# Where the first norm of a transformer trunk is applied: before three projections, or at their read-out

## The chip, the cores and the metric

The kernel runs on one core of a Trainium2 chip. Its time is device microseconds (us) of one execution; the median of three runs of the kernel before is 1945.42 us (1943.68 to 1946.59). The engines are named as the profile names them: PE multiplies matrices (PEld is its weight load, which overlaps), DVE does elementwise arithmetic, ACT does scaled copies and activations, POOL is a slower elementwise engine, and SP issues most DMA transfers from one queue, in order. Each engine works through its own instructions in the order in which the program holds them, and waits on semaphores for the others.

## The reference, cut to what matters

Two layers of a transformer with 512 latent and 256 context tokens of width 1024. Each layer starts like this (float32):

```python
def rms_norm(x, g):
    y = x * lax.rsqrt(jnp.mean(x * x, axis=-1, keepdims=True) + EPS)
    return y * g
def modulate(h, shift, scale):
    return h * (1 + scale) + shift

mod = silu(c) @ w_mod[l] + b_mod[l]          # one vector for latents, one for context
h   = modulate(rms_norm(x, norm1[l]), shift, scale)
z   = h @ w_in[l]                            # keys, values, queries of two kinds of attention, two gates
```

So for a token t and a channel c, `h = x[t,c] * r[t] * A[c] + m[c]`, where `r[t]` is the norm's factor of the token, `A[c] = norm1[c] * (1 + scale[c])`, and `m[c]` is the shift. `A` and `m` come in two sets, one for latents and one for context. A projection is `h @ W = r[t] * ((x*A) @ W) + m @ W`: the factor of a token can be taken out of the sum over channels, and the shift adds one number per output channel.

## The kernel before, in words

All tensors lie with the channels on 128 partitions and the tokens along the free axis: 8 tiles `x[k]` of 128 channels by 768 tokens (512 latents, then 256 context; spans s=0 and s=1). A float32 product is made of three matmuls: an operand is split into a high part rounded to `fp32r` and the low part that is left, and the terms high*high, low*high and high*low are added in PSUM. So a projection of 128 output channels takes 8 k by 3 matmuls over 512 columns and 8 by 3 over 256. The weights are split in the same way: `wh` by ACT (L640 for the stream of later weights, `wr` being the raw ones) and `wl` by POOL (L642).

The front of layer 0 is written in `Trunk.start`. It loads `x` (L840), squares each tile (`square`, ACT L844), adds the squares (`total`, DVE L847), sums them over the partitions by a matmul with ones (`means`, PE L853), adds eps, raises to the power -1/2 on POOL, and spreads the factor over all partitions with a matmul (`widen`, PE L870), so that it lies in PSUM as `rb`. Meanwhile the 8 column blocks of `w_mod` come in, two transfers of 512 KB each (`fetch`, L631, sixteen in all); for each k `sums` (PE L891), `parts` (ACT L897), `choose` (PE L901) and `settle` (DVE L906 and L909) make `A[:, :, k]` and `mod[:, :, k]`. Until there is something to multiply, PE runs matmuls that nothing uses (`warm`, L836). Then `scaled` (DVE L915) turns `x[k]` into x*A*r in place, `high` (ACT L920) writes `h` and `low` (DVE L924) writes `hl`. `multiply` (PE L950) runs the three projections whose weights are loaded first: gk (the keys), gv (the values) and gq0 (the first two query heads) of the grouped-query attention.

Behind the front come generators that read the projections out: `evac` of gk takes squares and a copy with the gain (ACT L1073, L1074) and sums the squares per head on PE (`st`, L1062); gv's is turned (`tv`, PE L1149). After them PE runs "fillers", projections that wait for nothing but weights and `h` (L655): nk0 (the keys of the first neighbourhood heads), nv0 (values), nq0 and so on; ACT L1200 and DVE L1201 read nk0's out. Between the fillers come the scores of the grouped-query attention, `sc` (L1305).

What sets the order: in the front, `Ops.run` plans a list of operations with costs in us, engine and priority (lower goes first), and sorts every engine's instructions by the planned starts. `FIRST` gives the order of the loads (x = a token tile, w = weights of a projection, b = small tables, a digit = the two halves of `w_mod` for that k). The fillers' instructions and loads are put in between and behind by a planner that reads the numbers in `PLAN[0]`. In PSUM, there are 8 banks; names `pj` are banks of projections. When the front is over, the mixing stage's pools g, t, s are laid over the same banks, in the order that `banks` gives, and a bank's new user waits until the old one has been read.

Of the kernel before, what the change touches and what calls it, by code (L numbers as in the profile page):

```python
# [12 lines left out]
F32 = mybir.dt.float32  # L13
# [7 lines left out]
P = 128  # L21
D = 1024
KB = D // P
# [21 lines left out]
for _n in ORDER:  # L45
    for _j in range(COLS[_n][1]):
# [32 lines left out]
         busy=12, ctx=0.0, vat=(1, 1), load=2, qt=2, rx=2, slow=(1.1, 1.2, 1), banks="gst", lead=(2, 1, 2), quiet=0.0, spared=0, all=False),  # L79
# [7 lines left out]
FIRST = "x x x x x x x x b 0 w 1 2 w 3 w 4 5 6 7"  # L87
AHEAD = 9

HOWW = "vvv"  # L90
START, HOP, LAND = 4.06, 0.15, 0.25
# [512 lines left out]
class Trunk:  # L604
# [207 lines left out]
    def start(self, h, pool, others):  # L812
# [8 lines left out]
        pick = pool.tile([P, 2], F32, tag="pick", name=self.name("pick"))  # L821
        nc.gpsimd.memset(cols, 0.0)
# [4 lines left out]
        tiles, x, sqs, rb, raws = {}, [], [], {}, {}  # L827
# [4 lines left out]
        add = todo.add  # L832
        chosen = self.ps("n", "ch")

# [11 lines left out]
        def total(k):  # L846
            nc.vector.tensor_tensor(sqs[0], sqs[0], sqs[k], op=ALU.add)  # L847

        def means(k):
            if k == 0:  # L850
                tiles["st"] = self.ps("n", "st")
            for t in range(nt):
                nc.tensor.matmul(  # L853
                    tiles["st"][:, t : t + 1], sqs[k][:, t * P : (t + 1) * P], self.ones, start=(k == 0 and t == 0),
                    stop=(k > 0), skip_group_check=True)

        def eps():
            r = tiles["r"] = pool.tile([P, nt], F32, tag="rs", name=self.name("rs"))
            nc.vector.tensor_scalar(r, tiles["st"][:, :nt], EPS, None, op0=ALU.add)
# [6 lines left out]
        def widen(s):  # L866
            a, b = spans[s]
            rb[s] = self.ps("n", "rb")
            for t in range(a // P, b // P):
                nc.tensor.matmul(  # L870
                    rb[s][:, t * P - a : t * P - a + P], tiles["r"][:, t : t + 1].to_broadcast([P, P]), self.ident,
                    start=True, stop=True)
# [38 lines left out]

        def scaled(k, s):
# [25 lines left out]
        def wlow(i, eng):  # L938
            weights[i].append(self.wpool.tile([P, D], F32R, tag="wl", name=self.name("wl")))
            (nc.gpsimd if eng == "g" else nc.vector).tensor_tensor(  # L940
                weights[i][2], weights[i][0], weights[i][1][:].bitcast(F32), op=ALU.subtract)

        def multiply(i, s, k):
            if k == 0:
                self.ahead[i, s] = self.ps("a", "pj")
            a, b = spans[s]
            ps, (raw, whi, wlo) = self.ahead[i, s][:, : b - a], weights[i]
            c = slice(k * P, (k + 1) * P)
            for n, (u, v) in enumerate(((whi, h[0]), (whi, h[1]), (wlo, h[0]))):
                nc.tensor.matmul(ps, u[:, c], v[k][:, a:b], start=(k == 0 and n == 0), stop=(k == KB - 1 and n == 2))  # L950
# [5 lines left out]
        last = None  # L956
        for what in FIRST.split():
            if what == "x":
                k = len(loaded)
                loaded.append(add("d", 0.92, token, (k,), [], 1))  # L960
                sq = add("a", 0.77, square, (k,), [loaded[k]], 1)
                if k < KB - 1:
                    last = add("v", 0.87, total, (k,), [last, sq], 1) if k else sq
                    continue
                last = add("p", 1.34, means, (0,), [last], 0)
                last = add("v", 0.08, eps, (), [add("p", 1.34, means, (KB - 1,), [last, sq], 0)], 0)
                wide = [
                    add("p", c, widen, (s,), [add("g", g, power, (s,), [last], 0)], 0)
                    for s, c, g in ((0, 0.86, 0.96), (1, 0.43, 0.63))]
# [1675 lines left out]
```

## Time and profile before

| what | value |
|---|---|
| median of three runs | 1945.42 us (1943.68 to 1946.59) |
| the profiled execution | 1943.38 us |
| its span in the trace | 1940.7 us |
| PE busy | 1909.2 us, 98% of the span |
| DVE busy | 1471.7 us, 76% |
| ACT busy | 937.8 us, 48% |
| POOL busy | 227.5 us, 12% |
| granted PE clock | 0.998 of full speed |

The times in the trace count from the start of the span. In a row of the timeline stand the start in us, the busy time in us, the engine, the line, the operation, out<-in, shapes, and the number of instructions that were put together; in brackets how long the engine was idle before it and what ended that. In a row of the windows stand the stretch, and for each engine its busy us and the number of its instructions, then the granted clock, the share of the DMA engines that was busy, and GB/s.

### The profile page before, as it was taken

The page shows a single profiled execution, that of the slowest core. Times are in us where ns is not written, and L with a number is a line of the kernel's source. Part 1 is how long each engine was busy: PE and PEld are TensorE (multiplying, and loading weights), DVE is VectorE, ACT ScalarE, POOL GpSimd, SP SyncE. Part 2 cuts the span into 40 slices and gives each one's busy share as a digit, 9 for nine tenths or more (in the row PEclk, how much of TensorE's full clock was granted, in tenths as well). Part 3 has the DMA queues.
Part 4 walks back from the last instruction along what each step waited for, and adds up shares of the span by engine and source line. Part 5 has one row for each costly group of instructions (what it writes and reads, how often), then busy time and mean ns, then how long its engine had stood idle before and what let it go on. Part 6 is the DMA issues. An engine that isn't in the chain of part 4 may idle for free.

```text
span 1940.7 us, 31522 instructions
## 1 busy us (share of the span) xinstructions
PE 1909.2 (98%) x12300; PEld 1764.5 (91%) x12300; DVE 1471.7 (76%) x2797; ACT 937.8 (48%) x1820; POOL 227.5 (12%) x132
## 2 busy tenths in 40 slices
PE   8999999999999999999999999999999999999998
PEld 6989999898889999999999888889988999999998
DVE  6468887769777888787868578898557587877785
ACT  4456666642226533343424345666553355544553
POOL 0432212214300000000000012132210000000000
PEclk9999999999999999999999999999999999999999
DMA  8121112235462134334443411022145532332332
GB/s 328 46 69 42 53 58 63 77 120 179 158 217 87 66 109 130 109 120 131 139 144 131 152 55 33 34 79 82 55 128 175 199 109 77 98 120 90 104 96 83
DMA packets 71670, 210.85 MB, mean 109 GB/s; under 512 B 8545, under 2 KB 10721, under 8 KB 71521
## 3 DMA queue, kind: packets, MB, share of 16 engines
q1 hardware_dynamic: 71520, 208.84, 32.9%
q8 instruction: 96, 1.57, 0.3%
q14 instruction: 54, 0.43, 0.1%
HBM read 196.75 MB, written 6.82 MB: 105 GB/s over the span
## 4 chain that ended last, share of the span: by engine, by line
PE 64%; DVE 5%; issue 1%; ACT 1%; DMA 1%; POOL 0%; SPq 0%; DVEq 0%; POOLq 0%; ACTq 0%
PE po L655 21%; PE qu L2021 14%; PE qv L2021 7%; PE pj L540 4%; PE qc L2021 3%; PE pj L655 3%; PE pf L655 3%; PE pp L655 2%; PE sc L540 2%; PE y L540 2%; PE tp L540 1%; PE pv L540 1%; ACT p L540 1%; DVE m L540 1%; DVE ptl L540 0%
## 5 line engine op out<-in xcount | busy, mean ns | idle before, releaser
L2021 PE MATMUL qu<-r,w 128*128 128x384 f32 (+1 forms) x1872 | 295.9, 310 | 0.3
L2021 PEld LDWEIGHTS qu<-r,w 128*128 128x128 f32 x1872 | 281.0, 189 | 5.0 <-DVE tt L2501 3.8
L1884 ACT ACTIVATE w<-wr 128x512 fp32r<-128x512 f32 x234 | 145.5, 625 | 107.6 <-DVE wr L2465 36.2
L655 PE MATMUL po<-ph,wh 128*128 128x512 f32 (+1 forms) x576 | 197.4, 343 | 0.0
L655 PE MATMUL po<-ph,wl 128*128 128x512 f32 (+1 forms) x576 | 196.8, 342 | 0.0
L655 PE MATMUL po<-pl,wh 128*128 128x512 f32 (+1 forms) x576 | 196.2, 341 | 0.0
L655 PE MATMUL pj<-h,wh 128*128 128x512 f32 (+1 forms) x512 | 182.1, 356 | 1.4 <-DVE ql L1256 1.1
L655 PE MATMUL pj<-h,wl 128*128 128x512 f32 (+1 forms) x512 | 176.8, 345 | 0.9 <-POOL wl L642 0.9
L655 PE MATMUL pj<-hl,wh 128*128 128x512 f32 (+1 forms) x512 | 176.6, 345 | 0.0
L1876 DVE SCALAR_TENSOR_TENSOR x<-po,G,x 128x256 f32<-128x256 f32 (+3 forms) x168 | 99.2, 596 | 100.7 <-PE po L655 99.7
L1888 DVE TENSOR_TENSOR w<-wr,w 128x512 fp32r<-128x512 f32 x234 | 159.3, 685 | 11.3 <-ACT w L1884 10.3
L640 ACT ACTIVATE wh<-wr 128x1024 fp32r<-128x1024 f32 (+1 forms) x109 | 101.3, 933 | 137.2 <-PE po L655 30.4
L2021 PE MATMUL qv<-r,w 128*128 128x384 f32 (+1 forms) x936 | 150.6, 309 | 0.3 <-ACT tt L2027 0.3
L2021 PEld LDWEIGHTS qv<-r,w 128*128 128x128 f32 x936 | 141.2, 190 | 0.5 <-ACT tt L2027 0.5
L782 POOL TENSOR_TENSOR rs<-rs,expo 128x2 f32<-128x2 f32 (+2 forms) x7 | 5.5, 784 | 1099.8 <-DVE rs L781 1099.8
L642 POOL TENSOR_TENSOR wl<-wr,wh 128x1024 fp32r<-128x1024 f32 (+1 forms) x47 | 103.5, 2205 | 229.2 <-ACT wh L640 228.9
L655 PEld LDWEIGHTS po<-ph,wl 128*128 128x128 f32 x576 | 108.2, 188 | 14.4 <-DVE wl L2192 0.4
L655 PEld LDWEIGHTS po<-pl,wh 128*128 128x128 f32 x576 | 108.5, 188 | 12.8
L655 PEld LDWEIGHTS po<-ph,wh 128*128 128x128 f32 x576 | 108.5, 188 | 12.8
L722 DVE CUSTOM_DVE_ANT_0 wr<-wr,crow 128x1024 f32<-128x1024 f32 x80 | 100.2, 1252 | 14.3 <-DMA wr<-wmodT 14.0
L655 PEld LDWEIGHTS pj<-h,wl 128*128 128x128 f32 x512 | 96.8, 189 | 13.4 <-POOL wl L642 1.3
L655 PEld LDWEIGHTS pj<-h,wh 128*128 128x128 f32 x512 | 97.0, 189 | 11.9 <-PE tp L1331 1.1
(341 smaller groups left out, 4705.7 us busy)
## 6 DMA issues: line engine op xcount, KB each, us to landing
wr<-wfi SPq DMA_DIRECT2D x88, 512.0 KB, 3.2
wr<-wmodT SPq DMA_DIRECT2D x80, 512.0 KB, 3.4
wr<-win SPq DMA_DIRECT2D x68, 512.0 KB, 3.7
wr<-wfo SPq DMA_DIRECT2D x64, 256.0 KB, 2.7
wr<-wo SPq DMA_DIRECT2D x26, 512.0 KB, 4.1
wr<-wmod SPq DMA_DIRECT2D x16, 512.0 KB, 9.9
wr<-wp SPq DMA_DIRECT2D x32, 256.0 KB, 2.9
x<-x SPq DMA_DIRECT2D x16, 384.0 KB, 7.1
```

The source lines that it names most:

```text
L540: ops[i]["run"](*ops[i]["args"], **ops[i]["kw"])
L640: nc.scalar.activation(hi, raw, AF.Copy)
L642: (eng or nc.gpsimd).tensor_tensor(lo, raw, hi[:].bitcast(F32), op=ALU.subtract)
L655: nc.tensor.matmul(ps[:, : b - a], u[:, c], v[k][:, a:b], start=(k == 0 and i == 0), stop=(k == nk - 1 and i == 2),)
L722: self.nc.vector.tensor_tensor_reduce(junk if s else w, w, crow[:, s], 1.0, 0.0, ALU.mult, ALU.add, self.mod[l][:, s, n : n + 1])
L782: nc.gpsimd.tensor_tensor(r[:, :nb], r[:, :nb], self.expo[:, :nb], op=ALU.pow)
L1876: self.nc.vector.scalar_tensor_tensor(x[j][:, f:u], ps[:, f - a : u - a], self.G[l][i][:, s, j : j + 1], x[j][:, f:u], op0=ALU.mult, op1=A ...
L1884: self.nc.scalar.activation(t[:, :n], src, AF.Copy)
L1888: self.nc.vector.tensor_tensor(t[:, n : 2 * n], src, t[:, :n].bitcast(F32), op=ALU.subtract)
L2021: nc.tensor.matmul(banks[bank], u[:, c], v, start=(first and k == 0 and i == 0), stop=(k == kn - 1 and i == 2), skip_group_check=True)
```

## The change

`FIRST` now interleaves loads of tokens with those of `w_mod` and weights. `multiply` (now L975) no longer takes `h`, but tiles made by two new functions: `upper` (ACT L923) and `lower` (DVE L930) split x*A, without `r`, into high and low parts. The context's high part lies in a tile `side` of 260 columns: 256 tokens, and four columns for the shift `m` of latents and context, high and low. So the shift's product with the weights comes out as columns 256 to 259 of the context's bank. All six banks (three projections, two spans) are open at once and are filled k by k. The factor is spread three times over two tiles of tokens and copied into SBUF (`settled`, ACT L878); it is then in the tile `rb`.

At the read-out, `shifts` (DVE L980, L981) adds the two columns of each shift, `normed` (DVE L987) multiplies a bank by the factor into a tile `up`, and `shifted` (ACT L992) adds the shift; the old read-outs take `up` in place of the bank. `h` is still needed by all fillers: `scaled` (DVE L940), `high` (ACT L945) and `low` (DVE L949) make it in the places where x*A stood, each piece when the three projections have used it. All `wl` of the first three projections are made on DVE, as before.

```diff
-         busy=12, ctx=0.0, vat=(1, 1), load=2, qt=2, rx=2, slow=(1.1, 1.2, 1), banks="gst", lead=(2, 1, 2), quiet=0.0, spared=0, all=False),
+         busy=14, ctx=8.0, vat=(1, 1), load=2, qt=2, rx=2, slow=(1.1, 1.2, 1), banks="gts", lead=(2, 1, 2), quiet=0.0, spared=0, all=False),
-FIRST = "x x x x x x x x b 0 w 1 2 w 3 w 4 5 6 7"
-AHEAD = 9
-START, HOP, LAND = 4.06, 0.15, 0.25
+FIRST = "b 0 x w w w 1 x 2 x x 3 x x x x 4 5 6 7"
+SIDE, SIDES = 260, 5
+AHEAD = 8
+START, HOP, LAND = 3.9, 0.15, 0.25
...
+        banks = {(i, s): self.ps("a", "pj") for i in range(3) for s in range(2)}
...
+        def settled(n):
+            if n == 0:
+                tiles["rb"] = pool.tile([P, T], F32, tag="qt", name=self.name("rb"))
+                for s, (a, b) in enumerate(spans):
+                    rb[s] = tiles["rb"][:, a:b]
+            nc.scalar.activation(tiles["rb"][:, n * 256 : n * 256 + 256], chosen[:, 256:512], AF.Copy)
...
+        def upper(k, s):
+            a, b = spans[s]
+            if s:
+                side[k] = pool.tile([P, SIDE], F32R, tag="side", name=self.name("side"))
+            to = side[k][:, 0:CTX] if s else h[0][k][:, a:b]
+            nc.scalar.activation(to, x[k][:, a:b], AF.Copy, scale=self.A[0][0][:, s, k : k + 1])
+            if s:
+                nc.scalar.activation(side[k][:, CTX : CTX + 2], mod[:, :, k], AF.Copy)
+
+        def lower(k, s):
+            a, b = spans[s]
+            hi = side[k][:, 0:CTX] if s else h[0][k][:, a:b]
+            nc.vector.scalar_tensor_tensor(
+                h[1][k][:, a:b], x[k][:, a:b], self.A[0][0][:, s, k : k + 1], hi.bitcast(F32),
+                op0=ALU.mult, op1=ALU.subtract)
+            if s:
+                nc.vector.tensor_tensor(
+                    side[k][:, CTX + 2 : CTX + 4], mod[:, :, k], side[k][:, CTX : CTX + 2].bitcast(F32), op=ALU.subtract)
...
         def multiply(i, s, k):
+            ps, (raw, whi, wlo) = banks[i, s], weights[i]
+            c = slice(k * P, (k + 1) * P)
+            if s:
+                pairs = (whi, side[k][:]), (whi, h[1][k][:, S:T]), (wlo, side[k][:])
+            else:
+                pairs = (whi, h[0][k][:, 0:S]), (whi, h[1][k][:, 0:S]), (wlo, h[0][k][:, 0:S])
+            for n, (u, v) in enumerate(pairs):
+                nc.tensor.matmul(
+                    ps[:, : v.shape[1]], u[:, c], v, start=(k == 0 and n == 0), stop=(k == KB - 1 and n == 2),
+                    skip_group_check=True)
+
+        def shifts(i):
+            nc.vector.tensor_copy(plus[:, i], banks[i, 1][:, CTX : CTX + 2])
+            nc.vector.tensor_tensor(plus[:, i], plus[:, i], banks[i, 1][:, CTX + 2 : CTX + 4], op=ALU.add)
+
+        def normed(i, s):
+            a, b = spans[s]
+            if not s:
+                scaled_up[i] = pool.tile([P, T], F32, tag="qt", name=self.name("up"))
+            nc.vector.tensor_tensor(scaled_up[i][:, a:b], banks[i, s][:, : b - a], rb[s][:, : b - a], op=ALU.mult)
+
+        def shifted(i, s):
+            a, b = spans[s]
+            u = scaled_up[i][:, a:b]
+            nc.scalar.activation(u, u, AF.Identity, bias=plus[:, i, s : s + 1])
+            self.ahead[i, s] = u
...
-            self.pbufs = dict(a=3, n=3, m=2)
+            self.pbufs = dict(a=6, n=1, m=1)
```

How the change moves instructions on three engines. **SP's queue**: `wr...<-wmod0` is half of a block of `w_mod`, `wr...<-win` is a raw weight of a projection (the fillers' in these rows), `x` a token tile. Before, all eight token tiles stand ahead of the first `w_mod`, and then:

```order
L631 DMA wr68_374<-wmod0 128x1024
L631 DMA wr93_668<-win 128x1024
L631 DMA wr102_702<-win 128x1024
L631 DMA wr70_387<-wmod0 128x1024
L631 DMA wr73_400<-wmod0 128x1024
L631 DMA wr76_418<-wmod0 128x1024
L631 DMA wr78_428<-wmod0 128x1024
L631 DMA wr80_446<-wmod0 128x1024
```

Now (the weight of the first filler, wr103, stands a few rows ahead of this piece):

```order
L631 DMA wr51_261<-wmod0 128x1024
L631 DMA wr106_737<-win 128x1024
L631 DMA wr109_743<-win 128x1024
L631 DMA wr116_809<-win 128x1024
L843 DMA x52_272<-x 128x768
L843 DMA x54_287<-x 128x768
L631 DMA wr57_297<-wmod0 128x1024
L631 DMA wr60_311<-wmod0 128x1024
L843 DMA x61_325<-x 128x768
L843 DMA x64_344<-x 128x768
L843 DMA x66_353<-x 128x768
L843 DMA x69_365<-x 128x768
```

Three weights of fillers that stood among or behind the last `w_mod` transfers stand ahead of six token tiles; the last token tile has 8 halves of `w_mod` and 7 weights ahead of it.

**DVE, at the end of the front**, between the last settle and the first read-out of nk0 (`pj112` is nk0's bank of latents, `pj23` to `pj26` are gv's and gq0's banks). Before, the last rows ahead of the read-outs are:

```order
L906 TENSOR_SCALAR A0_0_103<-ch20_137,more1_111,norms_sb_87 128x2
L909 TENSOR_SCALAR mod0_101<-ch20_137,more1_111 128x2
L924 SCALAR_TENSOR_TENSOR hl17_134<-x32_194,mod0_101,h16_133 128x256
L915 SCALAR_TENSOR_TENSOR x34_203<-x34_203,A0_0_103,rb48_265 128x512
L915 SCALAR_TENSOR_TENSOR x34_203<-x34_203,A0_0_103,rb50_272 128x256
L924 SCALAR_TENSOR_TENSOR hl19_136<-x34_203,mod0_101,h18_135 128x512
L924 SCALAR_TENSOR_TENSOR hl19_136<-x34_203,mod0_101,h18_135 128x256
L1048 STREAM_SHUFFLE sh118_792<-qg89_558 128x512
```

Now, where gq0's context bank `pj26` is read last:

```order
L981 TENSOR_TENSOR plus4_114<-plus4_114,pj24_141 128x2
L949 SCALAR_TENSOR_TENSOR hl20_137<-x69_365,mod0_101,h19_136 128x512
L949 SCALAR_TENSOR_TENSOR hl18_135<-x66_353,mod0_101,h17_134 128x256
L949 SCALAR_TENSOR_TENSOR hl20_137<-x69_365,mod0_101,h19_136 128x256
L987 TENSOR_TENSOR up98_680<-pj23_140,rb81_444 128x512
L987 TENSOR_TENSOR up98_680<-pj24_141,rb81_444 128x256
L980 COPY plus4_114<-pj26_143 128x2
L981 TENSOR_TENSOR plus4_114<-plus4_114,pj26_143 128x2
L987 TENSOR_TENSOR up99_686<-pj25_142,rb81_444 128x512
L987 TENSOR_TENSOR up99_686<-pj26_143,rb81_444 128x256
L1260 TENSOR_TENSOR k113_774<-pj112_749,k113_774 64x512
```

Between the last settle and nk0's read-out (now L1260) there were five elementwise passes over tiles; now there are the whole second half of the making of `h` and six read-outs.

**ACT, ahead of the fillers' weights** (L640 makes `wh104`, nk0's high weight). Before, it stands behind the first read-outs:

```order
L1074 ACTIVATE qg89_558<-pj84_515,qgain_99 128x512
L640 ACTIVATE wh94_670<-wr93_668 128x1024
L1073 ACTIVATE sq86_531<-pj88_554 128x256
L1074 ACTIVATE kg85_530<-pj88_554,gain_sb_88 128x256
L640 ACTIVATE wh103_704<-wr102_702 128x1024
```

Now:

```order
L945 ACTIVATE h13_130<-x61_325,mod0_101 128x512
L945 ACTIVATE h5_122<-x30_169,mod0_101 128x256
L945 ACTIVATE h7_124<-x45_236,mod0_101 128x256
L945 ACTIVATE h15_132<-x64_344,mod0_101 128x512
L945 ACTIVATE h9_126<-x52_272,mod0_101 128x256
L945 ACTIVATE h11_128<-x54_287,mod0_101 128x256
L945 ACTIVATE h17_134<-x66_353,mod0_101 128x512
L640 ACTIVATE wh104_733<-wr103_731 128x1024
L640 ACTIVATE wh107_739<-wr106_737 128x1024
L992 ACTIVATE up95_636<-up95_636,plus4_114 128x512
```

nk0's weight was split behind read-outs of the finished banks; it now stands behind `h17`, the high part of `h` for k = 6, which waits for DVE's `scaled` of that tile.

On PE the order within the front is now k by k over all six banks. Behind the front nk0 stood after the sums `st` and the turning `tv`; it now stands directly behind the last `multiply`, ahead of both. nk0's bank of latents takes the place of gk's bank of latents, and nk0's bank of context (`pj115`) takes the place of gq0's bank of context, `pj26`; the bank of nv0's first read-out takes the place of nk0's bank of latents.

123 lines of the change are left out of this document (65 added, 58 removed).

## The prediction

> **What bounds the kernel now.** I read the page's totals first, then the windows of the front, then the timeline of the rows that the change touches.
>
> ```profile
> span 1940.7 us, 31522 instructions
> PE 1909.2 (98%) x12300; PEld 1764.5 (91%) x12300; DVE 1471.7 (76%) x2797; ACT 937.8 (48%) x1820; POOL 227.5 (12%) x132
> ```
>
> PE is busy 98% of the span, so the time can only move by what PE waits: 31.5 us in all, and in the front what it does for nothing. The program behind the first 330 us is the same in both kernels' orders, so whatever the front gains or loses arrives at the end as it is.
>
> ```profile
> core 0: us, PE busy (x) PEld busy (x) DVE busy (x) ACT busy (x) POOL busy (x), PEclk, DMA share, GB/s
> 0.00:5.00 5.00, 1.34 (x6) 1.35 (x7) 1.44 (x13) 1.64 (x3) 0.52 (x5) 1.00 0.49 142
> 5.00:10.00 5.00, 5.00 (x27) 5.00 (x27) 1.92 (x2) 3.23 (x4) 0.00 (x0) 1.00 0.97 347
> 10.00:15.00 5.00, 5.00 (x47) 5.00 (x47) 4.16 (x7) 3.38 (x4) 0.00 (x0) 1.00 1.05 396
> 15.00:20.00 5.00, 5.00 (x52) 4.28 (x51) 1.40 (x2) 1.44 (x2) 1.83 (x2) 1.00 1.02 415
> 20.00:25.00 5.00, 4.07 (x49) 2.53 (x48) 2.59 (x8) 2.47 (x5) 0.00 (x0) 1.00 1.03 420
> 25.00:30.00 5.00, 4.83 (x40) 3.84 (x41) 4.63 (x12) 3.35 (x6) 0.00 (x0) 1.00 1.02 419
> 30.00:35.00 5.00, 4.10 (x37) 2.12 (x35) 5.00 (x12) 2.02 (x4) 0.00 (x0) 1.00 1.03 415
> 40.00:45.00 5.00, 5.00 (x38) 3.82 (x38) 4.96 (x13) 1.79 (x4) 0.00 (x0) 1.00 0.52 213
> 45.00:60.00 15.00, 15.00 (x95) 13.58 (x95) 3.67 (x7) 6.82 (x12) 4.58 (x2) 1.00 0.00 1
> 90.00:112.00 22.00, 20.75 (x134) 18.49 (x133) 17.07 (x40) 15.84 (x34) 7.20 (x3) 1.00 0.31 96
> 160.00:180.00 20.00, 19.42 (x140) 17.97 (x140) 16.52 (x41) 14.68 (x32) 4.65 (x2) 1.00 0.08 28
> 180.00:300.00 120.00, 119.94 (x824) 110.09 (x823) 101.20 (x205) 76.83 (x162) 32.47 (x19) 1.00 0.17 53
> ```
>
> The reader is to see three regimes. Up to 40 us the DMA engines are full (share about 1.0, some 415 GB/s), and PE waits on them. From 45 to 60 us PE has no gap at all and DVE is nearly idle: 3.67 us of 15. Later PE waits little: 1.25 us in 90 to 112, 0.58 in 160 to 180, 0.06 in 180 to 300, which is 1.89 together.
>
> ```profile
> 3.65 11.58 PE L836 MATMUL ch<-ident_sb 128*128 128x128 f32 x76 [3.65 <-DMA ident_sb<-ident]
> 9.14 4.74 ACT L844 ACTIVATE sq<-x 128x768 f32<-128x768 f32 x5 [0.29 <-DMA x<-x]
> 13.70 0.96 DVE L847 TENSOR_TENSOR sq<-sq,sq 128x768 f32<-128x768 f32 x1
> 15.07 2.74 PE L853 MATMUL st<-ones,sq 128*128 128x1 f32 x24
> 19.16 1.60 PE L870 MATMUL rb<-ident_sb,rs 128*128 128x128 f32 x12
> ```
>
> Before, the norm is done early: means at 15.07, the factor spread by 20.8. The 11.58 us of L836 ahead of it are dummies. That idle head is what the change could use; the price is that the factor comes later.
>
> **The change part by part. (A) The projections' end.** The last token tile now follows 8 halves of `w_mod` (4.19 MB) and 7 weights (3.67), itself and its seven fellows being 3.15 MB; with the identity (128x128 f32, 0.07 MB) that is 11.0 MB. The windows' rates, times 5 us each, give 0.71 + 1.74 + 1.98 + 2.08 + 2.10 + 2.10 = 10.7 MB by 30 us, so the last tile is there at about 31, plus 1.1: before, 3.22 MB had passed by 12.0 at these rates and the last square ran from 13.04 (9.14 + 4.74 less a fifth of it). With a square of 0.84 and a total of 0.96 behind it in DVE's queue, and some queueing of 1, the means start near 35 and, half as many as before (1.4 us), end near 36.5.
>
> What PE has left in its order then comes from these rows:
>
> ```profile
> 39.13 0.40 PE L950 MATMUL pj<-h,wl 128*128 128x512 f32 x1
> 39.36 0.40 PE L950 MATMUL pj<-h,wh 128*128 128x512 f32 x1
> 40.49 1.07 PE L891 MATMUL mp<-wr,cols 128*32 128x256 f32 x16
> 42.99 0.50 PE L901 MATMUL ch<-pick,part 128*128 128x2 f32 x4
> 53.00 0.28 PE L950 MATMUL pj<-h,wh 128*128 128x256 f32 x1
> 61.64 1.40 PE L1062 MATMUL st<-hones,sq 128*128 128x2 f32 x12
> ```
>
> A 512-column matmul takes 0.23 (39.13 to 39.36); one of 256 takes 0.12 (72 of them in 53.00 to 61.64); 260 columns cost 1/64 more on two of three, 0.1 us in all. One k is 9 x 0.23 + 9 x 0.12 = 3.15. Left are the multiplies of k = 3 to 7, four sums and chooses, and the spread: 5 x 3.15 + 4 x (1.07 + 0.50) + 1.60 = 23.6. So the projections end at 60.1 in place of 61.64: **-1.6 us**. Bounds: 0, if PE waits for the loads as it did in 20 to 35 (2.00 us of idle there); -5, if the four fillers' weights in the queue cost nothing (2.10 MB at 0.42 MB per us are 5.0 us).
>
> **(B) nk0's low weight.** DVE, idle before, now carries the splitting of x*A, the re-making of `h` and the read-outs:
>
> ```profile
> 43.53 0.28 DVE L906 TENSOR_SCALAR A<-ch,more,norms_sb 128x2 f32<-128x2 f32 x1
> 43.73 0.21 DVE L909 TENSOR_SCALAR mod<-ch,more 128x2 f32<-128x2 f32 x1
> 44.25 1.14 DVE L915 SCALAR_TENSOR_TENSOR x<-x,A,rb 128x512 f32<-128x512 f32 x2
> 42.11 1.11 ACT L920 ACTIVATE h<-x,mod 128x512 fp32r<-128x512 f32 x2
> 61.72 1.06 ACT L640 ACTIVATE wh<-wr 128x1024 fp32r<-128x1024 f32 x1 [1.55 <-PE pj L950]
> 62.85 2.40 POOL L642 TENSOR_TENSOR wl<-wr,wh 128x1024 fp32r<-128x1024 f32 x1 [0.45 <-ACT wh L640]
> 13.25 0.17 DVE L879 COPY more<-bmod_sb 128x8 f32<-128x8 f32 x1 [0.15 <-DMA bmod_sb<-bmod]
> ```
>
> A latent half and a context half of one tile together (the L915 row, x2) take 1.14 us, about 0.68 and 0.46; a settle takes 0.41 from its first start to its end; a copy of a few columns 0.17. The settle of k = 4 ends at 36.5 + 1.07 of sums + 0.69 (three matmuls in between) + 0.50 + 0.41 = 39.2. From there to `scaled` of k = 6 DVE's order holds 3 settles, 4 pairs of `lower` with their four small columns, 12 latent halves and 6 context halves: 1.2 + 4.6 + 0.7 + 8.2 + 2.8 = 17.5, that is 56.7 if it never waits. Then ACT's `h17` (0.7), ACT's `wh104` (1.06) and POOL's low weight (2.40) end at 60.9; with an estimated 0 to 1.5 us in which DVE waits for a settle, 60.9 to 62.4. PE arrives at 60.1 and can run two matmuls first. Cost **+1.3**, bounds 0 and 2.4.
>
> **(C) gq0's context bank.** From the settle of k = 4 to the last `normed` DVE's order has 3 settles, 20 pairs (4 lower, 8 scaled, 8 low), 4 small columns, and for the read-outs 3 pairs (`normed`, taken as L915's size) and 6 small rows: 1.2 + 22.8 + 0.7 + 3.4 + 1.0 = 29.1. So 68.3 if it never waits, 69.8 with the same 1.5. nk0's context matmuls reuse that bank. PE finishes nk0's latents at 60.1 + 1.3 + 24 x 0.23 = 66.9. Cost **+2.4**, bounds 1.0 and 3.5. What is late next: the context's 24 x 0.12 = 2.9 end at 72.2.
>
> ```profile
> 62.90 1.01 PE L1149 MATMUL tv<-ident_sb,vt 128*128 128x128 f32 x6
> 63.66 0.48 PE L655 MATMUL pj<-h,wh 128*128 128x512 f32 x1
> 69.22 0.28 PE L655 MATMUL pj<-h,wh 128*128 128x256 f32 x1
> 69.42 0.59 ACT L1200 ACTIVATE k<-pj 64x512 fp32r<-64x512 f32 x1 [4.42 <-PE pj L655]
> 70.04 0.68 DVE L1201 TENSOR_TENSOR k<-pj,k 64x512 fp32r<-64x512 f32 x1 [1.97 <-ACT k L1200]
> 72.09 1.40 PE L1062 MATMUL st<-hones,sq 128*128 128x2 f32 x12
> ```
>
> Before, `st` and `tv` took 2.0 us (61.64 to 63.66) and nk0 was done at 72.09; now, nk0 first and the two after it, 74.2. The sum so far is +2.1.
>
> **(D) nv0's first bank** is nk0's bank of latents, which ACT and DVE read. ACT has the first read-outs ahead of it: three `shifted` pairs, at L920's 1.11 some 3.3, and two squares and copies near 0.6 each; from 66.9 these last to 72 or so, and two pairs of 0.59 and 0.68 follow: 74.5 to 76.3 against PE's 74.2. Cost **+1.2**, bounds 0 and 2.0.
>
> **(E) The first scores and later.** They start at 89.4:
>
> ```profile
> L1305 PEld LDWEIGHTS sc<-kk,q x32: 187/188/192, 89.4 to 116.1; 128*128 128x128 f32 x32
> ```
>
> gk's `st` now comes at 72.2 and not at 61.64; the chain behind it (27.8 us) puts the scores at 100, 10.6 later. More of the filler matmuls are now ordered ahead of them: 21 of nv0 and 6 of nq0, some 3.9 us of PE. They fill the delay, but they are the work that covered the softmax's waits behind 90 us, where PE lost only 1.89. With the cover gone I count its own size, **+3.9**. Bounds: -1.9, if the new order has no wait there at all, and 7.3, the 10.6 less what B to D have already charged net of A.
>
> Edits costed at nothing: the spread has as many matmuls as before, in three pieces; `settled` on ACT (three copies of 256 columns, some 0.4 each) and the two side columns (0.17) lie under the DMA waits of 30 to 40 us and cost those amounts once each, 1.4 together, if ACT were on the path there.
>
> The sum: -1.6 + 1.3 + 2.4 + 1.2 + 3.9 = +7.2, against the profiled execution's 1943.38 us (span 1940.7, 2.7 around it): 1950.6. That execution was 2.0 under the median 1945.42, so **1952.6**.
>
> **The rivals.** (1) *Faster.* The fillers' loads cost nothing, because the queue is still draining when SP reaches them; means end near 31.5, five us earlier. Then DVE re-makes half of `h` (8 pairs x 1.14 = 9.1 us) in its idle time ahead of the last settle, its backlog ends at 68.3 - 9.1 = 59, under PE's 60, and B to E vanish: 1943.38 - 5 + 2.0 = 1940.4. For it: DVE was busy only 2.59 of 5 us in 20 to 25, so there is room for work that is ready early. Against: the DMA share is 1.0 from 10 us on; bytes ahead are time. It decides from the point at which the means end before 32.
>
> (2) *No change.* A to D come as computed but E is absorbed, since PE's order has other fillers: +3.3 to the start of the scores, then -1.9 to 0: about +2.4, 1947.8. For it: in 180 to 300 PE waited 0.06 of 120 us, so slack exists. Against: 90 to 112 already had 1.25 of waits.
>
> (3) *A colder PE.* In 5 to 10 us, after PE's late start, only 27 of the dummies passed, in 10 to 15 it was 47: they were slower at first, while PEclk read 1.00 in both. With projections that start on few tiles and wait for loads, stretches of slow matmuls could come back; at 47 - 27 = 20 dummies or 2.1 us per such stretch, one or two give 2 to 4 us on top: 1955.6.
>
> [...]
>
> **How the numbers follow.** My forecast (DVE's backlog becomes the bound for the first fillers) has 0.63, the colder PE 0.10, no change 0.17, faster 0.10. Within 0.2%, about what a measurement of this kernel can tell from no change, is 1941.5 to 1949.3. So faster 0.10, same 0.17, slower 0.73. The forecast's low end has B, D and E at nothing and C at 1.0: -0.6, or 1944.8; its high end is -1.6 + 2.4 + 3.5 + 2.0 + 7.3 = +13.6, or 1959. The range, 1945 to 1959, leaves out the faster case and half of the colder one's tail; the likeliest one's own is 1948 to 1957.
>
> **What would show it.** In the changed kernel's timeline: means on PE at 35 to 37 (A); the last `multiply` before 61; PE idle at nk0's third matmul, released by POOL's `wl` (B); PE idle some 2 us ahead of nk0's context matmuls, released by DVE's L987, with DVE without a gap from 40 to 69 (C); a wait at nv0's start on L1260 (D); first scores near 100 and PE idle of more than 2 us in 90 to 300 (E). I am wrong if the means end before 32, or if DVE's read-outs end before PE's last `multiply`.

## The result: slower by 0.9%, more than twice the forecast

The changed kernel takes 1965.3 us (median of 5 executions, 1961.2 to 1966.5), the kernel before beside it 1946.6 (1943.7 to 1950.6): a ratio of 1.0089, 95% interval 1.0073 to 1.0104. The forecast was slower, 1952.6 us, with a range up to 1959. The direction was right; the size, 18.7 us in place of 7.2, lies above the range.

### The profile after

The page of the changed kernel:

```profile
span 1963.2 us, 31547 instructions
PE 1914.9 (98%) x12266; PEld 1763.4 (90%) x12266; DVE 1492.0 (76%) x2834; ACT 951.5 (48%) x1853; POOL 225.9 (12%) x132
```

The totals tell nearly nothing: PE's busy time grew by 5.7 us though it does slightly fewer matmuls, and its share of the span is 98% as before. The place shows in the windows of the same kernel (columns as in the prediction):

```profile
25.00:30.00 5.00, 1.88 (x15) 0.91 (x13) 2.60 (x5) 2.90 (x5) 0.00 (x0) 0.98 1.03 406
30.00:35.00 5.00, 4.90 (x27) 3.69 (x28) 3.63 (x8) 3.71 (x6) 0.00 (x0) 0.68 1.03 408
60.00:70.00 10.00, 7.17 (x33) 5.36 (x32) 9.97 (x9) 6.84 (x11) 7.72 (x3) 1.00 0.33 111
70.00:80.00 10.00, 6.33 (x23) 5.13 (x24) 5.54 (x17) 7.24 (x14) 0.00 (x0) 0.54 0.12 47
90.00:112.00 22.00, 19.16 (x139) 17.99 (x138) 16.80 (x34) 10.74 (x21) 10.66 (x5) 1.00 0.15 49
112.00:160.00 48.00, 47.37 (x311) 42.61 (x310) 34.27 (x73) 29.50 (x59) 13.21 (x7) 1.00 0.17 50
180.00:300.00 120.00, 117.25 (x784) 105.47 (x783) 100.31 (x210) 79.04 (x164) 29.13 (x16) 1.00 0.16 50
```

The same two stretches of 10 us in the kernel before:

```profile
60.00:70.00 10.00, 10.00 (x64) 8.86 (x64) 1.97 (x6) 3.65 (x9) 7.02 (x4) 1.00 0.48 160
70.00:80.00 10.00, 10.00 (x87) 10.00 (x87) 6.81 (x12) 2.41 (x5) 5.87 (x3) 1.00 0.14 52
```

Between 60 and 80 us, where PE had no gap before, it is now busy 13.5 of 20 us, and in the second half at a granted clock of 0.54. DVE is busy all of 60 to 70 with nine instructions: over a microsecond on average, while its longest pieces there take 0.68 to 0.74 elsewhere in the trace. POOL is busy 7.7 us in the same window with three. Three rows of the timeline of that stretch, from POOL and DVE:

```profile
61.04 7.72 POOL L642 TENSOR_TENSOR wl<-wr,wh 128x1024 fp32r<-128x1024 f32 x3 [20.91 <-PE pj L975]
61.05 5.48 DVE L949 SCALAR_TENSOR_TENSOR hl<-x,mod,h 128x256 fp32r<-128x256 f32 x2
66.45 4.44 DVE L940 SCALAR_TENSOR_TENSOR x<-x,A,rb 128x256 f32<-128x256 f32 x5
```

Two `low` pieces (a context half and a latent half, put together in one row) take 5.48 us that need some 0.46 and 0.68, and five `scaled` pieces 4.44 that need 2.3. In the first row PE is what released POOL: the weights of the first projections are needed up to the last k, so three splits of fillers' weights run one behind the other from 61.0 on, in DVE's busiest stretch. Three splits ran as close together before (57.1 to 65.2), but beside a DVE that was busy 1.97 of 10 us. What PE waits for there, from the timeline of PE:

```profile
28.90 0.64 PE L897 MATMUL mp<-wr,cols 128*32 128x256 f32 x8 [2.65 <-DMA wr<-wmod]
36.77 1.40 PE L854 MATMUL ch<-ones,sq 128*128 128x1 f32 x12
61.94 0.39 PE L655 MATMUL pj<-h,wh 128*128 128x512 f32 x1
63.49 0.51 PE L655 MATMUL pj<-h,wl 128*128 128x512 f32 x1 [0.93 <-POOL wl L642]
70.92 0.80 PE L655 MATMUL pj<-h,wh 128*128 128x512 f32 x1 [2.82 <-ACT h L945]
72.68 0.79 PE L655 MATMUL pj<-hl,wh 128*128 128x512 f32 x1 [0.97 <-DVE hl L949]
75.69 0.55 PE L655 MATMUL pj<-h,wh 128*128 128x256 f32 x1 [1.79 <-DVE up L987]
82.82 0.36 PE L1281 MATMUL pv<-wh,h 128*128 128x256 f32 x1
105.84 0.47 PE L655 MATMUL pj<-h,wh 128*128 128x512 f32 x1 [2.84 <-DVE v L1291]
```

The sum by places, in the two profiled executions. The projections end at 61.94 in place of 61.64: +0.3. nk0 waits 0.93 for its low weight, 2.82 and 0.97 for `h` and `hl` of k = 7, 1.79 for the bank: +6.5. nk0 with `st` and `tv` took 61.64 to 72.09 = 10.45 before; now 61.94 to 82.82 = 20.88, so beside the waits 3.9 us more: slow matmuls. At nv0's start the kernel is +10.7 (82.82 - 72.09; gq0's `st` and a spread, which stood ahead of nv0, now stand behind it). The scores of the second layer, which stand in the identical part of the program, show what had gathered by then (the tile view of `sc`; the first of the two numbers behind the durations is the first start):

```profile
L540 PE MATMUL sc<-kk,q x128: 274/386/504, 1186.2 to 1305.8; 128*128 128x512 f32 x64, 128*128 128x256 f32 x64
```

```profile
L540 PE MATMUL sc<-kk,q x128: 274/386/504, 1202.2 to 1322.6; 128*128 128x512 f32 x64, 128*128 128x256 f32 x64
```

Before (first row) and after (second): +16.0 at 1186 us. So 5.3 came between nv0 and there: 90 to 300 us hold 6.2 us of PE idle now (2.84, 0.63 and 2.75 by the windows; 160 to 180 has none) and held 1.9 before. The profiled execution then lost 5 us more around 1320, which the last part of the experiments takes up.

### The profile page after: what moved, and what is told of

The parts are those of the page before. It is cut to its first block, busy times and chain, and to the rows that moved or that the text cites. A ratio compares the mean times of both kernels' runs of the same rounds, so it can differ in the third digit from the quotient of the medians.

```text
span 1963.2 us, 31547 instructions
## 1 busy us (share of the span) xinstructions
PE 1914.9 (98%) x12266; PEld 1763.4 (90%) x12266; DVE 1492.0 (76%) x2834; ACT 951.5 (48%) x1853; POOL 225.9 (12%) x132
## 4 chain that ended last, share of the span: by engine, by line
PE 61%; DVE 6%; issue 2%; DMA 1%; ACT 1%; POOL 0%; SPq 0%; DVEq 0%; POOLq 0%; ACTq 0%
PE po L655 20%; PE qu L2080 13%; PE qv L2080 7%; PE pj L540 4%; PE qc L2080 3%; PE pj L655 3%; PE pf L655 3%; PE pp L655 2%; PE y L540 1%; PE sc L540 1%; PE pv L540 1%; PE tp L540 1%; DMA wr<-wmodT 1%; DVE m L540 1%; ACT p L540 1%
## 5 line engine op out<-in xcount | busy, mean ns | idle before, releaser
L1943 ACT ACTIVATE w<-wr 128x512 fp32r<-128x512 f32 x234 | 145.5, 625 | 106.8 <-DVE wr L2524 36.2
L640 ACT ACTIVATE wh<-wr 128x1024 fp32r<-128x1024 f32 (+1 forms) x109 | 101.3, 933 | 133.5 <-PE po L655 28.8
```

Of the source, the lines that this page charges most:

```text
L640: nc.scalar.activation(hi, raw, AF.Copy)
L1943: self.nc.scalar.activation(t[:, :n], src, AF.Copy)
```

## The experiments

Theory H: DVE is late with the re-making of `h`, because the factor is late, and POOL's splits hold up DVE's instructions while they run; the rest is lost behind nv0 by the fillers' new order. Rival L: the late loads are the whole cost. Rival P: the new numbers in `PLAN` are. Where a time "at the second layer's scores" is given, it is that row's first start, against 1186.2 of the kernel before; a comparison of whole times carries the spread of executions too.

### 1. The old order of loads

```diff
-FIRST = "b 0 x w w w 1 x 2 x x 3 x x x x 4 5 6 7"
+FIRST = "x x x x x x x x b 0 w 1 2 w 3 w 4 5 6 7"
```

> The changed kernel with the old order of loads (all token tiles first, then w_mod and the weights). Theory H (DVE's backlog, and its being held up while POOL splits weights): the factor is there 15 us earlier, DVE re-makes much of h before the last settle, so of the 11 us lost by the start of nv0 about 7 come back, but two of the three weight splits still hold DVE; what is lost behind 100 us stays: about 1956 us, 9 under the changed kernel, still about 10 over the one before. Rival L (the late loads are the whole cost): at or under the kernel before, 1941 to 1947. Rival P (the new numbers in PLAN cost it, the front is level): no better than the changed kernel, 1963 to 1966.

1954.5 us, ratio to the kernel before 1.0041 (1.0022 to 1.0060): 8.3 us over it, some 11 under the changed kernel. L alone falls, P alone falls. The ten executions lie from 1946.5 to 1963.0 us, and they order themselves roughly by their mean granted clock: 0.998 for the fastest, 0.991 for the slowest. The profiled one has one of the low clocks; its window from 20 to 30 us and a row of its PE timeline:

```profile
20.00:30.00 10.00, 8.93 (x45) 6.35 (x45) 3.53 (x11) 3.73 (x9) 0.86 (x1) 0.55 1.03 410
```

```profile
66.73 0.50 PE L655 MATMUL pj<-h,wl 128*128 128x512 f32 x1 [0.97 <-POOL wl L642]
```

PE ran ten microseconds at half clock (0.55) though it had work in 8.93 of them, and the projections ended at 65.1, later than in any other kernel here. The wait for nk0's low weight stays.

### 2. The old numbers in PLAN

```diff
-         busy=14, ctx=8.0, vat=(1, 1), load=2, qt=2, rx=2, slow=(1.1, 1.2, 1), banks="gts", lead=(2, 1, 2), quiet=0.0, spared=0, all=False),
+         busy=12, ctx=0.0, vat=(1, 1), load=2, qt=2, rx=2, slow=(1.1, 1.2, 1), banks="gst", lead=(2, 1, 2), quiet=0.0, spared=0, all=False),
```

> The changed kernel with the old numbers in PLAN (busy 12, ctx 0, banks gst), so st and tv stand ahead of nk0 again and the fillers behind have their old order. Theory H: PE's waits move from nk0 to st and tv but stay as long (10 to 12 us up to 80 us), since DVE's work is the same; the waits behind 100 us go: about 1959 us, 6 under the changed kernel. Rival P: the old numbers bring back nearly all, 1946 to 1950. Rival L: no difference to the changed kernel, 1963 to 1966.

1959.5 us, 1.0064 (1.0042 to 1.0086), as H expected. The waits only move; from PE's timeline:

```profile
64.25 2.72 PE L1121 MATMUL st<-hones,sq 128*128 128x2 f32 x12 [2.05 <-ACT sq L1132]
75.48 1.54 PE L1208 MATMUL tv<-ident_sb,vt 128*128 128x128 f32 x6 [8.51 <-ACT vt L1188]
```

With `st` and `tv` ahead of nk0, PE waits 10.6 us for read-outs in place of 6.5 for nk0's data. The order with nk0 first was the better cover for the late read-outs, and cost more further on: from nv0 to 300 us PE waits 1.8 us here, in the same three places as in the kernel before (number 5 shows both lists).

### 3. POOL writes but does not read

```diff
-        (eng or nc.gpsimd).tensor_tensor(lo, raw, hi[:].bitcast(F32), op=ALU.subtract)
+        self.nth = getattr(self, "nth", 0) + 1
+        if self.nth <= 3:
+            nc.gpsimd.memset(lo[:].bitcast(F32), 0.0)
+        else:
+            (eng or nc.gpsimd).tensor_tensor(lo, raw, hi[:].bitcast(F32), op=ALU.subtract)
```

> The changed kernel, but POOL's first three splits of fillers' weights (nk0's and nv0's two) are fills with zero: POOL works in the same places on the same tiles, but reads nothing; the low parts of these three weights are left out of the result. Theory H: none of DVE's instructions takes over 1 us between 60 and 70 us (three took 2.6 to 2.9), DVE's read-outs end near 69 in place of 75.5, PE's waits ahead of nk0's context shrink from 6.5 to about 3.5 us and the slow matmuls with them: 5 to 8 us under the changed kernel, 1957 to 1960. Rival (backlog alone; the long DVE entries are an effect of how they are recorded): only the 0.9 us in which PE waited for nk0's low weight goes, 1964.

1961.7 us, 1.0077 (1.0060 to 1.0095): 3.6 under the changed kernel, less than the 5 to 8 expected. The fills take 0.96 us each and lie beside DVE's work from 59.9 to 63.0. DVE's rows of the stretch:

```profile
60.95 1.14 DVE L953 SCALAR_TENSOR_TENSOR hl<-x,mod,h 128x256 fp32r<-128x256 f32 x2
62.01 2.33 DVE L944 SCALAR_TENSOR_TENSOR x<-x,A,rb 128x256 f32<-128x256 f32 x5
66.28 0.88 DVE L953 SCALAR_TENSOR_TENSOR hl<-x,mod,h 128x256 fp32r<-128x256 f32 x2 [1.94 <-ACT h L949]
```

The same two pieces that took 5.48 us take 1.14, and the five that took 4.44 take 2.33: 6.45 us less. That is the whole stretching, so it was real and went with POOL's subtractions; beside the fills, which read nothing and are shorter (0.96 in place of 2.39 to 2.82), nothing was stretched. Of these 6.45, DVE gives 1.94 back: it now waits for ACT, whose `h` of k = 4 stands behind fillers' weights and gk's read-out. The read-outs end at 71.0 in place of 75.5, and PE still waits

```profile
71.16 0.55 PE L659 MATMUL pj<-h,wh 128*128 128x256 f32 x1 [2.27 <-DVE up L991]
```

2.27 us for gq0's bank, about the 2.4 that the prediction had for it.

Since this kernel and the changed one had been timed on different chips, both ran once more on one:

> The changed kernel as it is, on one chip with the next one, so that the two can be compared within a few us. Theory H and its rival both: 16 to 19 us over the kernel before; three of DVE's instructions between 60 and 70 us at 2.6 to 2.9 us again.

> The third experiment's kernel (POOL's first three splits of fillers' weights as fills with zero; the low parts of these weights are left out of the result) on one chip with the changed kernel. Theory H: 2.5 to 5 us under it. Rival (backlog alone): at most 1 us under it.

1966.8 us (ratio 1.0103, 1.0086 to 1.0119) for the changed kernel, 1959.9 (1.0076, 1.0059 to 1.0093) for the other: the medians are 7.0 us apart, more than H's 2.5 to 5 and far from the rival's 1. The intervals of the ratios overlap by a little, so the size is rough; 0.9 us of it is the wait for nk0's low weight, which the fills take away too. At the second layer's scores they stand at 1204.5 and 1197.7.

### 4. Without DVE's part of the re-making

```diff
-                t = add("v", u, scaled, (k, s), [wide[s], use[k, s]], (3 + k * 0.1, 3.45 + k * 0.05)[s])
+                t = use[k, s]
                 t = add("a", hi, high, (k, s), [t, *(done[i, s, k] for i in range(3))], (3 + k * 0.1, 3.45 + k * 0.05)[s])
-                add("v", lo, low, (k, s), [t], (3 + k * 0.1, 3.45 + k * 0.05)[s])
```

> The changed kernel without DVE's part in re-making h (scaled and low are left out, 16 pairs, about 18 us of DVE; ACT still writes the high parts, from the unscaled tokens, so all later layers compute with wrong h). Theory H: read-outs follow the last multiply directly, PE's waits between 62 and 80 us shrink from 6.5 to about 2 us, no slow matmuls: 8 to 9 under the changed kernel, 1956; the rest of the loss lies in front of 62 us and behind 100. Rival L (late loads): the projections end no earlier and nothing else changes, 1963 to 1966. Rival P: less than 3 us under the changed kernel.

This kernel leaves out DVE's `scaled` and `low`, so what it computes behind them is something else; only its times are read. 1959.3 us, 1.0069 (1.0047 to 1.0090): 6 under the changed kernel, 2 to 3 less than H expected. The waits ahead of nk0's last k and of its bank are gone; the 0.93 for the low weight stays, and 1.45 at nv0's start is new. So even with 18 us less on DVE the kernel is 13 us slower than before: DVE's backlog and the hold explain PE's waits between 62 and 80 us but not the rest. (This execution also ended its projections later, at 64.3.)

### 5. The new numbers in PLAN alone, on the kernel before

```diff
-         busy=12, ctx=0.0, vat=(1, 1), load=2, qt=2, rx=2, slow=(1.1, 1.2, 1), banks="gst", lead=(2, 1, 2), quiet=0.0, spared=0, all=False),
+         busy=14, ctx=8.0, vat=(1, 1), load=2, qt=2, rx=2, slow=(1.1, 1.2, 1), banks="gts", lead=(2, 1, 2), quiet=0.0, spared=0, all=False),
```

> The kernel before with one part of the change alone: the new numbers in PLAN (busy 14, ctx 8, banks gts); front and projections as before. Theory H now says that about 5 of the 16 us come from the fillers' order behind 100 us: nq0 waits some 3 us for nv0's read-out as in the changed kernel, and further waits of about 1 us follow up to 310: 4 to 8 us over the kernel before, 1950 to 1954. Rival Q (that order is harmless by itself, and its waits come from DVE's backlog in the front): within 2 us of the kernel before, 1944 to 1948.

1949.9 us beside 1947.3: 1.0012 (0.9998 to 1.0026), which is between the two expectations and no proof of a loss. Its trace is clearer than its time:

```profile
94.95 0.59 PE L655 MATMUL pj<-h,wh 128*128 128x512 f32 x1 [2.84 <-DVE v L1232]
```

nq0 waits 2.84 us for nv0's read-out, to the hundredth as in the changed kernel, with no backlog on DVE. So this wait belongs to the order and not to the late factor, as H had it. The others do too. In the list of PE's waits from nv0 to 300 us (us in total, times, longest) this run has

```profile
PE pj L655 <- DVE v L1232: 2.8, 1, 2.8
PE y L1341 <- DVE ptl L1282: 1.9, 2, 1.0
PE pj L655 <- DVE ql L1256: 0.5, 1, 0.5
PE tp L1461 <- DVE z L1275: 0.3, 1, 0.3
PE tp L1331 <- DVE ptl L1282: 0.2, 1, 0.2
```

and the changed kernel has the same five with the same numbers, 5.7 us together. The kernel before has, as number 2 with the changed front has,

```profile
PE pj L655 <- DVE ql L1256: 0.9, 1, 0.9
PE y L1341 <- DVE ptl L1282: 0.6, 1, 0.6
PE pj L655 <- DVE v L1232: 0.3, 1, 0.3
```

1.8 us. So these waits go with the numbers in `PLAN`, whichever front stands ahead of them: 3.9 of the 5.3 us behind nv0. The other 1.4 were not taken apart.

### 6 and 7. Both undone, and the read-outs moved forward

Number 6 has the edits of 1 and 2. Number 7 adds to it:

```diff
-                        [*halves[s], *wdone[i], *([done[i, s, k - 1]] if k else [])], 4 + 0.1 * k)
+                        [*halves[s], *wdone[i], *([done[i, s, k - 1]] if k else [])], 4 + 0.1 * k + (0.25 if i == 2 and k > 4 else 0))
...
-            soon = (1, 3.9, 4.3)[i]
+            soon = (1, 1.1, 4.3)[i]
```

> The changed kernel with both the old order of loads and the old numbers in PLAN. Theory H: the waits behind 100 us go (as in the second experiment), the factor is early (as in the first), and what is left is that st and tv wait some 4 to 5 us for read-outs which stand behind the re-making of h: 2 to 4 us over the kernel before, 1948 to 1950. Rival (the two undone parts overlap, each giving back the same wait): no better than the better of the two, 1954.

> The sixth experiment's kernel, with gv's read-out ranked ahead of the re-making of h, and the last three k of gq0's multiplies put behind gk's and gv's, so that PE has work while gk is read out. Theory H: the waits at st and tv shrink to about 2 us: as the kernel before or up to 2 us under it, 1944 to 1946. Rival (moving the factor costs more than the order of the read-outs can hide): 1948 or more.

Number 6: 1952.5 us beside 1947.3, 1.0026 (1.0007 to 1.0045); its profile shows the waits expected, 2.07 and 0.41 at `st` and 2.08 at `tv`. It is only 2 to 3 us better than number 1 (2.0 by the medians, 0.0015 by the ratios), within the spread, and misses H's 1948 to 1950, so the times alone do not tell H from the rival. Number 7: 1949.5, 1.0011 (1.0000 to 1.0023); in its profile

```profile
62.54 0.61 PE L1121 MATMUL st<-hones,sq 128*128 128x2 f32 x4 [0.55 <-ACT sq L1132]
64.22 1.54 PE L1208 MATMUL tv<-ident_sb,vt 128*128 128x128 f32 x6 [1.07 <-ACT vt L1188]
```

the waits are 1.6 us in all, and the last multiply ends before 61.6. This is the best version with the factor at the read-out; it comes level with the kernel before at most. H expected up to 2 us under it, and that did not come. Part of its lead over number 6 may be the clock: the profiled execution of number 6 has a mean granted clock of 0.994 and ended its projections at 64.4, that of number 7 has 0.997 and ended them at 61.05. No version here beats the kernel before.

### 8. More dummies in the kernel before

```diff
         def means(k):
...
+            for n in range(8 if k else 0):
+                warm()
...
         def widen(s):
...
+            for n in range(3):
+                warm()
...
         def choose(k):
...
+            for n in range(4 if k < 2 else 0):
+                warm()
```

> The kernel before with more unused matmuls on PE between 15 and 27 us: 8 behind the means, 3 behind each spread, 4 behind the first two chooses, where PE mostly waits. In three of the other profiles the granted clock went to half within 3 us of the means, for 7 to 10 us. Theory C (the thin matmuls of that stretch, of 1 to 2 columns, are what lets the clock fall): no half-speed stretch before 60 us, times of the executions closer together, mean granted clock 0.997 in place of 0.9955, and 1 to 3 us under the kernel before. Rival (the stretches come by chance or from elsewhere, and the dummies only stand in the way): same spread, 0 to 2 us over the kernel before.

1944.4 us beside 1945.5: 1.0002 (0.9990 to 1.0014). The mean granted clock of its executions is 0.9965 against 0.9955, and from 12 to 32 us its profile shows no slow matmuls (16 matmuls of the sums take 1.07 us at 19.13, as at 17.74 in the kernel before; in number 1, at half clock, they took 1.94 at 24.36), but the time does not move measurably. Unclear; the cause of the half-speed stretches in the front stays open.

### 9. Numbers 2 and 3 together

> The second and the third experiment together: the changed kernel with the old numbers in PLAN, and POOL's first three splits of fillers' weights as fills with zero (the low parts of these weights are left out of the result). Theory H: tv waited 8.5 us in the second experiment for a read-out that stood behind the three held instructions; that wait shrinks by 4 to 6.5 us, and the half-speed stretch around 64 to 81 us with it: 4 to 8 us under the second experiment's kernel, 1952 to 1956. Rival (both gave back the same wait): no better than the second alone, 1958 to 1960.

1954.5 us, 1.0059 (1.0036 to 1.0082); in medians 5 under number 2, but the two ran on different chips and the ratios' intervals overlap. The trace carries the verdict:

```profile
71.43 1.54 PE L1212 MATMUL tv<-ident_sb,vt 128*128 128x128 f32 x6 [4.45 <-ACT vt L1192]
```

The wait of 8.51 us at `tv` is 4.45: the hold by POOL was worth 4.06 us here, at another place of PE's order, with the same DVE instructions ahead. The first wait at `st` is 2.05 in both.

### What the runs leave open

Some profiled executions lose 2 to 5 us around 1320 us, in the part that is the same in all kernels: the changed kernel (both profiles), numbers 1, 2, 3, 5 and 7; the others lose about 1 or nothing (4, 6, 8, 9, the second profile of 3). Rows of the changed kernel and the one before, shifted by the 16 us:

```profile
1316.00:1336.00 20.00, 16.98 (x103) 14.62 (x101) 16.51 (x28) 11.81 (x23) 6.79 (x4) 0.91 0.09 32
```

```profile
1300.00:1320.00 20.00, 19.29 (x138) 17.55 (x137) 18.65 (x38) 13.94 (x27) 6.82 (x4) 1.00 0.04 15
```

PE idles 3 us and the clock dips to 0.91. The timeline of the changed kernel there shows POOL's hold once more:

```profile
1320.12 2.39 POOL L540 TENSOR_TENSOR wl<-wr,wh 128x1024 fp32r<-128x1024 f32 x1
1320.57 2.35 DVE L540 TENSOR_SCALAR p<-p,rc 128x768 f32<-128x768 f32 x1
1322.83 2.34 POOL L540 TENSOR_TENSOR wl<-wr,wh 128x1024 fp32r<-128x1024 f32 x1 [0.32 <-ACT wh L540]
1323.03 2.80 DVE L540 TENSOR_SCALAR p<-p,rc 128x768 f32<-128x768 f32 x1
1325.89 0.33 PE L540 MATMUL tp<-ident_sb,p 128*128 128x128 f32 x1 [2.40 <-DVE p L540]
```

and of the one before:

```profile
1303.76 1.39 DVE L540 TENSOR_SCALAR p<-p,rc 128x768 f32<-128x768 f32 x1
1305.26 0.62 DVE L540 TENSOR_SCALAR p<-p,rc 128x768 f32<-128x768 f32 x1
```

A scaling that takes 0.62 us alone takes 2.35 and 2.80 when a weight split begins just ahead of each of the two, and PE waits 2.40 for the second. The same wait of 2.4 stands in all seven profiles that lose, and in none of the others. Why the two fall together in some executions stays open; how far the front is behind does not decide it (number 7, 2.8 us late at the second layer's scores, has it; the second profile of 3, 11.5 late, does not).

## Why the prediction was right or wrong

**What bounds the kernel, and the direction.** Right in the main: the loss arises in the front and up to 300 us, and DVE, idle there before, becomes what PE waits for. Two things differ: 3.9 us of it are slow matmuls, in which PE counts as busy, and it does not arrive quite as it is, since more is lost around 1320 us in the part that is the same.

**A, the projections' end: -1.6 forecast, +0.3 measured.** The means ended at 38.2, the forecast was 36.5, and that is the whole error: from there to the projections' end PE took 23.8 us, the sum 23.6. The queues in front of them were longer than the 1 us allowed, on ACT for the squares and on DVE for the totals, which also stand behind a settle:

```profile
32.07 2.77 ACT L847 ACTIVATE sq<-x 128x768 f32<-128x768 f32 x3
34.19 2.01 DVE L850 TENSOR_TENSOR sq<-sq,sq 128x768 f32<-128x768 f32 x2
```

The last square ends at 34.8 in place of 33, the last total at 36.2 in place of 35. What PE lost ahead of that, 2.65 us of waiting for `w_mod` behind 26 us and 3.4 us at half clock (0.68 in 30 to 35), cost nothing here: when it was through with k = 3, it ran unused matmuls from 36.10 to the means. The bound of 0 was nearly it.

**B, nk0's low weight: +1.3 forecast, 0.93 measured.** Right, by nearly the chain that was given: `h17` ended at 59.7, and the split of the weight then waited 0.18 us for PE, which freed its buffer. That the size fits is in part luck, since both ends came later than in the sum: PE at 61.9 in place of 60.1, the low weight at 63.4 in place of 60.9 to 62.4.

**C, the bank: +2.4 forecast, 5.6 of waits and about 3.9 of slow matmuls measured. This is the step that failed.** DVE's 29.1 us were made from durations that rows of the kernel before show for a DVE that works alone; what POOL's splits would add was put at nothing. It was 6.45 us on three instructions, and the last read-out ended at 75.5 in place of 68.3 to 69.8. With the hold off (number 3), the read-outs ended at 71.0 and the wait for the bank was 2.27: the mechanism was right, the durations were not. That 2.27 comes so near 2.4 is in part luck, because PE was late too (68.9 in place of 66.9). The hold was there to be seen in the profile of before: the group of one rope step, and the rows of POOL and DVE at its last start,

```profile
L1051 DVE TENSOR_TENSOR qg<-qg,sh x4: 692/693/2872, 57.1 to 183.8; 128x512 f32<-128x512 f32 x4
```

```profile
183.78 2.39 POOL L642 TENSOR_TENSOR wl<-wr,wh 128x1024 fp32r<-128x1024 f32 x1
183.84 2.87 DVE L1051 TENSOR_TENSOR qg<-qg,sh 128x512 f32<-128x512 f32 x1 [1.18 <-POOL sh L1049]
```

(in the first row minimum, median and maximum, then first and last start). One execution of four took 2872 ns, the one that began just behind a weight split of POOL. The prediction priced POOL's split only as a time that nk0 waits for, never as something that DVE would wait for. `h` and `hl` of k = 7 were no term at all; with the hold off (number 3) PE still waits 0.53 and 0.35 for them.

In the trace two `low` pieces and a `scaled` with the factor in SBUF each began up to 0.51 us behind the start of a split, and ended 0.28 to 0.55 behind its end: 61.05 to 63.72 (the split 61.04 to 63.43), 63.64 to 66.53 (63.38 to 65.98), and 66.45 to 69.04 (65.94 to 68.76). Beside a POOL that only writes (number 3) none was held. `rb` lay in PSUM before the change and lies in SBUF now; whether `scaled`, 2.59 us in one piece of the 4.44 us row, would have been held with `rb` in PSUM, no run shows.

**Rival 3, the colder PE.** Given a tenth as a separate course, it was part of the main one: when PE had been without a matmul from 68.1 on, the clock fell to half at 70.7, for 10.2 us. The extra 3.9 us beside nk0's waits are its price, near the 2 to 4 forecast for it. The profile of before held a case that speaks for it: from 545 to 549 us PE is busy 1.56 of 4 us, and from 549 to 552.3 its granted clock is 0.50.

**D, nv0's first bank: +1.2 forecast, nothing measured.** nv0 followed `tv` without a gap: PE came so late that the bank was free. In number 4, where PE came earlier, the wait was 1.45.

**E, later waits: +3.9 forecast, 5.3 measured.** Right in place: the waits from nv0 to 300 us grew by 3.9. But the forecast had them follow from gk's late `st`, which takes the cover away, and priced them by the size of that cover. Number 5 has the same waits without any lateness, so the new order makes them by itself, and that the 3.9 agrees is luck. The last 2.7 us of the 18.7 are not placed: they are within the spread of executions, and both profiles of the changed kernel have the loss around 1320, which no term was for.

**Rival 1, faster,** was to decide at means before 32 us. Number 1 has them at 16.4 and is still slower: with the factor early the kernel comes nearer (by 11 us), but the projections don't end 5 us earlier (65.1 in number 1; 61.05 in number 7, whose granted clock was 1.00 from 20 to 30 us).

## What to carry to other kernels

A duration taken from a trace holds for the company that the instruction had there (a `low` piece took 0.47 us alone and 2.67 beside a split): before an elementwise engine's backlog is summed, look whether another engine's work will move into the same stretch, and whether the group's maximum, not its median, has something to say of that. Work in the background that was harmless beside an idle engine was not so here beside a busy one: the three weight splits ran as close together before the change (57.1 to 65.2 us), beside a DVE that was busy 1.97 of 10. Taking a factor out of a product removes it from the critical start, but if the scaled operand is needed again later, its making has only been moved to where DVE must also read out.

## What the runs showed of the hardware

Beside POOL's subtraction of two SBUF tiles of 128x1024 (2.39 us at 61.04 in the changed kernel) three of DVE's instructions with two SBUF inputs took longer: 0.47 became 2.59 and 2.67, 0.74 became 2.89. Beside POOL's fill of the same tile (0.96) none did. DVE's scaling of one tile of 128x768 (around 1320 us) took longer beside the subtraction too: 0.62 became 2.35 and 2.80. And once POOL was the one that was late: at 57.09 us of the kernel before both began together, DVE's step took its usual 0.69, and the split 2.96.

Half-speed stretches of PE came in pieces of 3.4, 6.8, 10.2 and once 17 us: 3.4 from 29.8 us in the changed kernel (0.50 in 30.0 to 33.0), 6.8 in number 3 (0.66 in 70 to 80), 10.2 from 70.7 in the changed kernel, 10.2 from 18.8 in number 1, 17.1 from 64.1 in number 2. In number 1 PE's records showed work in nearly nine of ten microseconds of it (8.93 of 10 from 20 on), though some 3 us of that was thin work: matmuls of two columns (1.01 us at 21.00), or onto 32 rows (1.94 at 24.36). In the changed kernel the clock fell 2.6 us behind the last matmul (68.1 to 70.7). That thin work is the cause is not shown: the kernel before has the same kind of work at a clock of 1.00 from 15 to 30 us (the sums at 17.74 and 21.04).

The mean granted clock of an execution goes with its time: over 75 executions of the kernel before it lies between 0.993 and 0.998, and their medians fall from 1951.1 us (0.993) over 1947.4 (0.995) to 1941.9 (0.998), some 1.7 us for each 0.001. By an estimate from these lengths that is about what half clock costs by itself: one stretch of 3.4 us at half speed takes 0.0009 off the mean, and holds a busy PE up by 1.7 us. Of the changed kernel's 18.7 us, 0.002 in mean clock (0.9936 against 0.9956) is then some 3; these are no further loss, but mostly the slow matmuls of part C seen from another side.
